# Seven block products for the long set's outputs, with their weights split ahead into DRAM, in an encoder layer on one Trainium2 core

## The chip, the core and the metric

The kernel runs on one core of a Trainium2 chip. A core has five engines with a queue of instructions each, which run beside one another and wait for each other through semaphores: TensorE (PE in the profile) does matrix products, VectorE (DVE) and ScalarE (ACT) do element-wise work on up to 128 rows at once, GpSimd (POOL) does element-wise work too, and SyncE (SP) only starts transfers. Any of SP, ACT and POOL can start a transfer (DMA). An instruction that waits holds up all that stand behind it in its engine's queue. The metric is the device time of one execution in microseconds (us); the kernel before takes 2188.45 us, the median of three runs.

## The reference

One encoder layer in fp32 is applied to a long set of 1024 rows (`x_prompt`, called A in the code) and a short set of 512 rows (`x_sample`, called B), each of 1024 columns. Per set:

```
h      = rms_norm(x) * pre_w                       # row by row
cols   = h @ w_in                                  # 1024 -> 12304 columns
y_m    = mlstm(q, k, v, gates) * sigmoid(o) * silu(z)       # 1024 wide
y_a    = dilated_attention(3 groups of q, k, v) * silu(z_a) #  512 wide
merged = sig(g_A) * (y_m @ w_proj_m) + sig(g_B) * (y_a @ w_proj_a)
out    = merged @ w_out
x      = x + rms_norm(out) * post_w
```

Everything after the two mixers, so `y_m @ w_proj_m`, `y_a @ w_proj_a`, the gates, `merged @ w_out`, the norm and the sum with x, is called the outputs here. It is these of the long set that the change rewrites.

## The kernel before

Every fp32 operand of a product is **split** into a high part (a copy rounded to the type that TensorE takes at full rate) and a low part (operand less high part), and each product is three matmuls: high by high, high by low, low by high (`mm3`, L230). ScalarE makes high parts by a copy, VectorE low parts by a subtraction. A matmul is 128x128 by 128x512. A step of the output work is one `mm3`.

The program has stages, and TensorE's order in the later ones is written by the program itself.

1. The value columns of the long set come first.
2. **The pairs**: the other columns of the long set, two units of 128 columns at a time, as seven block products in place of eight (`unit_pair`, L788, in the order m1 m6 m2 m7 m5 m4 m3 on TensorE; a product is 12 matmuls, a pair 84). There are 38 pairs: 12 `att`, then four times conv, conv, gate, then 8 `zo`, 2 `az`, and 4 gate pairs at the end. The weights of a pair go into buffers `pw_raw` (a ring of 4) through SP, and are split into `phla` (a ring of 2: the operands of m1, m2, m6, m5) and `phlb` (a ring of 2: one buffer for m7 and m4, one for m3). The names `c`, `pu2` and `pu3` are the pair's sums, made by VectorE from the PSUM tiles `d` (L808 takes m2 and L809 m6, L819 takes m3, the last product). The order of ScalarE, VectorE, POOL and SP in this stage is set by a scheduler, from priorities and its own cost table.
3. **The short set's inputs**: its rows are transposed on TensorE (L348), split into `H0` to `H3` (L354 on ScalarE, L355 on VectorE), and multiplied by `w_in` unit by unit (`dense` tiles). Their weights arrive in `wraw0` and `wraw1`, and are split into three pairs of places `wh`, `wl` (L285, L296, L302). The low parts of the first three units are made by POOL. SP's order is the program's own.
4. **Mixers with fill**: mLSTM and attention of A and B run one after another, each laid out in rounds, and between the rounds the class `Fill` puts steps of the dense work: the short set's inputs, then the outputs of A and of B. `STEPS` says how many steps go into which mixer. The steps of A's outputs are 128 for `w_proj_m`, 64 for `w_proj_a` and 128 for `w_out`, in two halves of rows (`branches` and `final`). Beside them the split of the next half's rows of y_m and y_a is made by `along`, which advances a generator once in so many steps. From L2540 on weights are issued by POOL's queue.
5. The mixed attention of B (`combine`), B's own projection and its `w_out` close the program. The residual `x` is loaded (`xo`), VectorE multiplies and adds to it (L2271), and SP stores it.

## Time and profile before

| what | value |
|---|---|
| median of three runs | 2188.45 us (2188.39 to 2188.65) |
| span of the profiled execution, first to last instruction | 2185.1 us |
| what lies around that span, against the median run | 3.4 us |
| TensorE busy | 2173.5 us, 99% |
| VectorE, ScalarE, POOL busy | 1460.8, 1085.1, 704.2 us |
| moved by DMA | 395.62 MB, mean 181 GB/s |
| granted TensorE clock | 0.999 |

The span is the only time that the profiled execution has of its own, so the 3.4 us are the difference from the runs' median. In the tables of windows below, a row gives the busy time of each engine in a stretch of 50 us, and how many instructions it ran. In a timeline a row gives start, length, engine, line and names; what stands in brackets at its end is the idle time before the instruction and what ended it. A matmul's own length in the profile overlaps with the next one's, so what a matmul costs is read from the distance between starts, or from their number in a stretch. Line numbers are those of the kernel before; in the kernel after, the same statement stands some lines further down (L764 becomes L766, L296 becomes L298, L285 becomes L287, L354 becomes L356, L808 becomes L858, L2145 becomes L2202).

### The profile page before, as it was taken

To read this page: it belongs to the slowest core of one execution; us is meant where nothing else is said; L and a number is where in the kernel's file an instruction comes from. 1 tells how busy PE (TensorE), PEld (TensorE's weight loads), DVE (VectorE), ACT (ScalarE), POOL (GpSimd) and SP (SyncE) were. 2 spreads that over 40 slices of the span, in tenths; PEclk is the share of its full clock that TensorE was granted. 3 is DMA by queue.
4 is the path that set the end of the run, shared out by engine and by line. 5 is a ranking of instruction groups with operands and counts; after the bars stand their busy time and mean duration, and the time that the engine had idled before them with its cause. 6 is when DMAs were issued, how large, how long until landed. Compare 5 with 4: busy or idle time off the path is not lost.

```text
span 2185.1 us, 33611 instructions
## 1 busy us (share of the span) xinstructions
PE 2173.5 (99%) x11626; PEld 1857.3 (85%) x11626; DVE 1460.8 (67%) x2927; ACT 1085.1 (50%) x2228; POOL 704.2 (32%) x989
## 2 busy tenths in 40 slices
...
GB/s 139 193 139 73 146 162 144 227 110 116 107 115 114 75 82 97 135 216 261 202 164 225 175 167 262 240 241 196 203 233 278 248 288 205 229 261 187 242 240 106
DMA packets 205748, 395.62 MB, mean 181 GB/s; under 512 B 36393, under 2 KB 117993, under 8 KB 205578
## 3 DMA queue, kind: packets, MB, share of 16 engines
...
## 4 chain that ended last, share of the span: by engine, by line
PE 97%; DVE 1%; ACT 1%; DMA 1%; issue 0%; POOL 0%; DVEq 0%; POOLq 0%; ACTq 0%
PE d L233 14%; PE d L235 14%; PE d L234 14%; PE dense L233 13%; PE dense L234 13%; PE dense L235 13%; PE lg L1801 2%; PE pt L1831 2%; PE o L1874 1%; PE num L233 1%; PE num L235 1%; PE num L234 1%; PE num L1494 1%; PE o L1853 1%; PE a L1201 1%; PE kv L233 1%
## 5 line engine op out<-in xcount | busy, mean ns | idle before, releaser
L233 PE MATMUL dense<-H,wh 128*128 128x512 f32 x664 | 269.3, 406 | 0.0
L234 PE MATMUL dense<-H,wh 128*128 128x512 f32 x664 | 260.3, 392 | 0.0
L235 PE MATMUL dense<-H,wl 128*128 128x512 f32 x664 | 260.2, 392 | 0.0
L233 PE MATMUL d<-Hh,phla 128*128 128x512 f32 x608 | 236.5, 389 | 0.0
L235 PE MATMUL d<-Hh,phla 128*128 128x512 f32 x608 | 236.5, 389 | 0.0
L234 PE MATMUL d<-Hl,phla 128*128 128x512 f32 x608 | 236.5, 389 | 0.0
L302 DVE TENSOR_TENSOR wl<-wraw,wh 128x1024 fp32r<-128x1024 f32 (+1 forms) x121 | 150.8, 1248 | 57.9 <-ACT wh L296 57.8
L235 PE MATMUL d<-Hh,phlb 128*128 128x512 f32 x456 | 177.4, 389 | 0.0
L233 PE MATMUL d<-Hh,phlb 128*128 128x512 f32 x456 | 177.4, 389 | 0.0
L234 PE MATMUL d<-Hl,phlb 128*128 128x512 f32 x456 | 177.4, 389 | 0.0
L296 ACT ACTIVATE wh<-wraw 128x1024 fp32r<-128x1024 f32 (+1 forms) x124 | 128.1, 1036 | 62.1 <-PE dense L234 24.3
L235 PEld LDWEIGHTS dense<-H,wl 128*128 128x128 f32 x664 | 124.7, 188 | 28.1
L782 POOL TENSOR_TENSOR psum_w<-pw_raw 128x512 f32<-128x512 f32 x38 | 56.7, 1492 | 271.1 <-DMA pw_raw<-w_in 259.9
L1820 DVE CUSTOM_DVE_ANT_0 ls<-lg,bias 128x256 f32<-128x256 f32 (+2 forms) x240 | 78.7, 350 | 90.3 <-PE lg L1801 61.7
L233 PEld LDWEIGHTS dense<-H,wh 128*128 128x128 f32 x664 | 125.0, 188 | 16.4 <-issue 1.2
L234 PEld LDWEIGHTS dense<-H,wh 128*128 128x128 f32 x664 | 125.2, 189 | 14.7
L235 PEld LDWEIGHTS d<-Hh,phla 128*128 128x128 f32 x608 | 114.1, 188 | 23.7
L234 PEld LDWEIGHTS d<-Hl,phla 128*128 128x128 f32 x608 | 114.1, 188 | 23.7
L233 PEld LDWEIGHTS d<-Hh,phla 128*128 128x128 f32 x608 | 114.1, 188 | 23.7
L800 POOL TENSOR_TENSOR psum_w<-pw_raw,psum_w 128x512 f32<-128x512 f32 x38 | 49.3, 1298 | 254.2 <-DVE phla L764 254.2
L1824 ACT ACTIVATE ls<-ls,nm 128x256 f32<-128x256 f32 (+1 forms) x192 | 87.3, 456 | 70.2 <-DVE nm L1822 47.0
L233 PE MATMUL d<-v,Hh 128*128 128x484 f32 (+1 forms) x336 | 121.3, 361 | 0.1
...
## 6 DMA issues: line engine op xcount, KB each, us to landing
pw_raw<-w_in SPq DMA_DIRECT2D x76, 512.0 KB, 3.9
wraw<-w_in SPq DMA_DIRECT2D x63, 512.0 KB, 4.4
aqk_a<-pwk SPq DMA_DIRECT2D x32, 512.0 KB, 6.7
wraw<-w_pm POOLq DMA_DIRECT2D x24, 512.0 KB, 5.9
wraw<-w_out POOLq DMA_DIRECT2D x24, 512.0 KB, 3.7
Q<-aqk_a SPq DMA_DIRECT2D x20, 512.0 KB, 6.3
...
aqk_b<-sw SPq DMA_DIRECT2D x36, 256.0 KB, 7.2
```

Of the source, the lines that this page charges most:

```text
L233: nc.tensor.matmul(out, lh, rh, start=start, stop=False, **kw)
L234: nc.tensor.matmul(out, lh, rl, start=False, stop=False, **kw)
L235: nc.tensor.matmul(out, ll, rh, start=False, stop=stop, **kw)
L296: high = nc.scalar.activation(hi[:, :n], raw[:, :n], AF.Copy)
L302: low = (self.lows or nc.vector).tensor_sub(lo[:, :n], raw[:, :n], hi[:, :n].bitcast(F32))
L782: self.nc.gpsimd.tensor_add(s[:, 0], ws[1][:, 0], ws[1][:, 1])
L800: nc.gpsimd.tensor_sub(s[:, 1], wa[:, 1], s[:, 1])
L1201: nc.tensor.matmul(p[:, c - c0], kT[:, ct, c * P:(c + 1) * P], qT[:, ct, c * P:(c + 1) * P], start=ct == 0, stop=ct == 1)
L1801: nc.tensor.matmul(lg[:, hh], q[hh][:, qs], z.rearrange("p (n j) -> p n j", j=P)[:, pair], start=z is k[hh], stop=z is not k[hh])
L1820: nc.vector.tensor_tensor_reduce(out=ls[rows, hh], in0=ts["lg"][hh][rows, of], in1=bt[rows, hh, by], scale=1.0, scalar=NEG, op0=OP.add, op ...
L1824: self.held = self.held[-3:] + [nc.scalar.activation(ls[:, hh], ls[:, hh], AF.Exp, bias=nm[:, hh:hh + 1], accum_out=ot[:, 128 + hh:129 + hh])]
L1831: nc.tensor.transpose(pp[:, hh * nk + x], ts["ls"][:, hh, x * P:(x + 1) * P], self.ident)
```

## The change

The outputs of the long set are computed as seven block products each for `w_proj_m` and `w_out`, 512 rows by 512 columns by 512 deep, so that each takes 112 steps in place of 128; `w_proj_a` keeps its 64. The weights that these need (five quadrants' combinations, each split) are prepared in the pairs stage: `pre_quads` loads quadrants of both weight matrices, makes the combinations on POOL, splits them into a `phlb` buffer and writes both parts to a DRAM tensor `pre`; `pre_plain` does the same for the unchanged weights (`w_proj_a`, and B's own). Sixteen calls of the first kind stand behind the 8 zo, the 4 gate and the 4 last pairs, twenty of the second behind the others. In the output stage a unit's weights are two transfers of 512 KB from `pre` straight into a split place. The combinations of the operands (sums of row blocks, the jobs of `combined` in the code), their splits and the sums of the products are done by VectorE and ScalarE between the steps (`outputs`). The residual is no longer loaded: eight transfers from DRAM to DRAM copy `x_prompt` into `y_prompt` during the conv pairs, and the finished rows are added there by accumulating transfers on POOL's queue. `STEPS` is redistributed, and the split of B's rows (`branches`, L2202) now runs in every second step of the last 28 of the long set's `w_out`.

```diff
             self.fetch(len(self.ready) + 1)
-            self.ready.append(self.net.split_w(*self.raws[len(self.ready)]))
+            raw = self.raws[len(self.ready)]
+            self.ready.append(self.net.split_w(*raw) if raw else self.net.load_pre(self.srcs[len(self.ready)][1]))
             self.fetch(len(self.ready) + self.net.deep)
 
     def fetch(self, n):
         while len(self.raws) < min(n, len(self.srcs)):
-            self.raws.append(self.net.load_w(*self.srcs[len(self.raws)]))
+            src = self.srcs[len(self.raws)]
+            self.raws.append(self.net.load_w(*src) if len(src) != 2 else None)
 
...
+    def pre_split(self, x, units, sb, to):
+        nc, n = self.nc, x.shape[1]
+        hl = sb.tile([P, 2, 2, BLK], F32R, name="phlb", bufs=2)
+        nc.scalar.activation(hl[:, 0, :n], x, AF.Copy)
+        nc.vector.tensor_sub(hl[:, 1, :n], x, hl[:, 0, :n].bitcast(F32))
+        for j, u in enumerate(units):
+            y = hl.rearrange("p z a c -> p z (a c)") if to is None else hl[:, :, j]
+            dst = self.pre[u] if to is None else self.pre[u, :, :, to]
+            nc.sync.dma_start(dst.rearrange("z p c -> p z c"), y.bitcast(F32))
+    def pre_plain(self, u, src, sb):
+        w = sb.tile([P, 2, BLK], F32, name="pw_raw", bufs=4)
+        self.nc.sync.dma_start(w, src.rearrange("p (a c) -> p a c", a=2))
+        self.pre_split(w, [u], sb, None)
+    def pre_quads(self, i, sb):
+        nc, q = self.nc, self.a["w_q"]
+        u, c = i // 4, slice(i // 2 % 2 * BLK, (i // 2 % 2 + 1) * BLK)
+        at = lambda *js: [4 * QUADS.index(j) + u for j in js]
+        ws = []
+        for b in range(2):
+            w = sb.tile([P, 2, BLK], F32, name="pw_raw", bufs=4)
+            nc.sync.dma_start(w, q[2 * b:2 * b + 2, u, :, c].rearrange("q p c -> p q c"))
+            ws.append(w)
+        wa, wb = ws
+        s = sb.tile([P, 2, BLK], F32, name="psum_w", bufs=2)
+        nc.gpsimd.tensor_add(s[:, 0], wb[:, 0], wb[:, 1])
+        nc.gpsimd.tensor_sub(s[:, 1], s[:, 0], wa[:, 0])
+        if i % 2 == 0:
+            self.pre_split(wa, at(0, 1), sb, c)
+            self.pre_split(s, at(4, 5), sb, c)
+        else:
+            nc.gpsimd.tensor_sub(wb[:, 0], wa[:, 0], wb[:, 0])
+            nc.gpsimd.tensor_sub(wa[:, 1], wa[:, 1], s[:, 1])
+            self.pre_split(wb, at(6, 3), sb, c)
+            self.pre_split(wa[:, 1:], at(7), sb, c)
+    def load_pre(self, u):
+        hi, lo = self.wsplit.pop(0)
+        self.wsplit.append((hi, lo))
+        for z, x in enumerate((hi, lo)):
+            self.loaded = self.side.dma_start(x[:, :1024].bitcast(F32), self.pre[u, z])
+        return hi[:, :1024], lo[:, :1024]
...
+    def outputs(self, T, before):
...
+        def divide(into, key, at, x):
+            hi, lo = at
+            nc.scalar.activation(hi, x, AF.Copy)
+            sub(lo, x, hi.bitcast(F32))
+            into[key] = at
+        def third(k):
+            sub(M["a1"][:, k], M["b1"][:, k], M["a1"][:, k])
+        def second(k):
+            add(M["a0"][:, k], M["a0"][:, k], M["a1"][:, k])
...
+        def proj_m(weights):
+            fill = weights.__self__
+            ring = [M["even"], slots("H0") + slots("H1")]
+            for n in range(2):
+                gate(n)
+            u, x = four("H3"), None
+            pm = M["pm"] = {(0, 0): four("H2"), (0, 1): u}
+            uses = [(i, k) for i in range(7) for _ in range(4) for k in range(4)]
+            jobs = combined("m", ring, uses)
...
+            for i in range(7):
+                for g in range(2):
+                    w = weights()
+                    if t == 0:
+                        self.more_places(fill, [[self.ring.tile([P, RING], F32R, name=f"wraw{z}") for z in range(2)]])
+                    for j in range(2):
+                        ps = self.dense()
+                        for k in range(4):
+                            give(jobs, t)
+                            give(late, t)
+                            c = slice(j * S + k * P, j * S + (k + 1) * P)
+                            self.mm3(ps, (w[0][:, c], w[1][:, c]), made["m", i, k], k == 0, k == 3)
+                            if k == 3:
+                                evict(i, 2 * g + j, ps)
+                            t += 1
+                            yield
+            assert not jobs
+            give(late, t, 99)
...
+            def close(b, t, ys):
+                s = ss[b][:, t]
+                nc.vector.scalar_tensor_tensor(s[:, 5:6], s[:, 0:1], 4 * EPS * D, s[:, 1:2], op0=OP.add, op1=OP.add)
+                nc.gpsimd.tensor_tensor(s[:, 6:7], s[:, 5:6], self.mhalf[:, :1], op=OP.pow)
+                r0 = b * S + t * P
+                for h, y in enumerate(ys):
+                    c = slice(h * S, (h + 1) * S)
+                    nc.vector.scalar_tensor_tensor(y, y, s[:, 6:7], pw[:, c], op0=OP.mult, op1=OP.mult)
+                    nc.gpsimd.dma_start(T.y[r0:r0 + P, c], y, accum_op=OP.add)
...
+        units = self.along(before, begin, 1)
+        units.append(Unit([("pre", 4 * i + g) for i in range(7) for g in range(2)], proj_m))
+        units.append(Unit([("pre", PRE_A + i) for i in range(KT // 2)], proj_a))
+        return units, Unit([("pre", 4 * i + 2 + k) for i in range(7) for k in range(2)], final)
...
-        return (self.along(before, lambda: self.split(T, b, 0, [(odd, 0, 1), (odd, 2, 1)], yb, 2 if len(before) > 1 else 3), 3)
-                + self.along([Unit([(a["w_pm"][ct],) for ct in range(KT)], proj_m)],
+        return (self.along(before, lambda: self.split(T, b, 0, [(odd, 0, 1), (odd, 2, 1)], yb, 3), 2, 86)
+                + self.along([Unit([("pre", PRE_M + ct) for ct in range(KT)], proj_m)],
                              lambda: self.split(T, b, 8, [(1 - odd, 1, 2)], ya, 3), 4)
-                + [Unit([(a["w_pa"][ct],) for ct in range(KT // 2)], proj_a)])
+                + [Unit([("pre", PRE_A + ct) for ct in range(KT // 2)], proj_a)])
 
...
-STEPS = (316, 260, 192, 290, 86)
+STEPS = (316, 260, 192, (6, 4.5), 22, 57)
+QUADS = (0, 1, 5, 6, 3, 4, 7)
+PRE_M, PRE_A, PRE_O, PRE = 28, 36, 40, 48
...
+                        if kind in ("zo", "gate"):
+                            N.pre_quads(i if kind == "zo" else 8 + i // 2, sb)
+                        elif plain:
+                            N.pre_plain(*plain.pop(0))
+                        if kind == "conv":
+                            with tc.issue_after(N.split_end.ins):
+                                t = rows.pop(0)
+                                nc.sync.dma_start(A.y[P * t:P * (t + 1)], A.x[P * t:P * (t + 1)])
...
                     c = N.unit_pair(N.pair_weights(u, u + 1, sb)[0], H, sb, cp, ps)
+                    N.pre_quads(12 + j, sb)
...
-            finals = [N.final(*x) for x in ((A, 0), (A, 1), (B, 0))]
-            units = short[:-4] + N.branches(A, 0, 0, short[-4:])
-            units += N.branches(A, 1, 1, finals[:1]) + N.branches(B, 0, 0, finals[1:2]) + finals[2:]
+            last = N.final(B, 0)
+            first, final = N.outputs(A, short[-4:])
+            units = short[:-4] + first + N.branches(B, 0, 0, [final]) + [last]
...
-                fill.stage(STEPS[4], 3 * B.n + 6)
+                fill.stage(STEPS[4], 4)
                 fill(2)
                 next(mixed)
                 fill(2)
+                fill.stage(STEPS[5], 3 * B.n + 2)
```

Three places show how instructions move. Names with a number are one buffer each.

**SP's queue at the end of the pairs stage.** Before, the last loads of pair weights, then those of the short set's inputs (`wraw`):

```order
L777 DMA pw_raw_7019<-w_in 128x1024 [waits DMAHW3_49,Pool_49]
L777 DMA pw_raw_7021<-w_in 128x1024 [waits DVE_49]
L1039 DMA gb512_7161<-gb4 128x1 [waits DMAHW3_49,Pool_49]
L285 DMA wraw0_7146<-w_in 128x1024 [waits DMAHW4_49,PE_49]
L285 DMA wraw1_7147<-w_in 128x1024 [waits DMAHW5_49]
L285 DMA wraw0_7146<-w_in 128x1024 [waits DMAHW6_49,DMAHW4_49,Pool_49]
L285 DMA wraw1_7147<-w_in 128x1024 [waits DMAHW7_49,DMAHW5_49,Pool_49]
```

After, the splits of the last two calls of `pre_quads` are written out first (`phlb_7539`, `phlb_7544`):

```order
L799 DMA pre_82<-phlb_7397 128x2x512 [waits DMAHW6_49,DVE_49]
L799 DMA pre_82<-phlb_7397 128x2x512 [waits DMAHW7_49]
L799 DMA pre_82<-phlb_7539 128x2x512 [waits DMAHW0_49,DVE_49]
L799 DMA pre_82<-phlb_7539 128x2x512 [waits DMAHW1_49]
L799 DMA pre_82<-phlb_7544 128x2x512 [waits DMAHW2_49,DVE_49]
L1089 DMA gb512_7570<-gb4 128x1 [waits DMAHW4_49,DMAHW3_49,Pool_49]
L287 DMA wraw0_7555<-w_in 128x1024 [waits PE_49]
L287 DMA wraw1_7556<-w_in 128x1024 [waits DMAHW5_49]
L287 DMA wraw0_7555<-w_in 128x1024 [waits DMAHW6_49,DMAHW4_49,Pool_49]
```

The last `pre` write waits for VectorE's subtraction into `phlb_7544`, and the loads of `wraw` stand behind it.

**VectorE's queue around the split of m7's operand in a conv pair that follows a gate pair.** Before (`phlb_4172` is the operand, `d_4136` the last product of the pair ahead of it):

```order
L764 TENSOR_TENSOR phla_4179<-psum_w_4182,phla_4179 128x1024 [waits Activation_49]
L816 TENSOR_TENSOR c_4048<-pu3_4027,d_4120 128x512 [waits PE_49]
L764 TENSOR_TENSOR phlb_4172<-pw_raw_4176,phlb_4172 128x1024 [waits DMAHW4_49,Activation_49]
L819 TENSOR_TENSOR c_4047<-pu2_4026,d_4136 128x512 [waits DVE_49,PE_49]
L764 TENSOR_TENSOR phlb_4173<-psum_w_4182,phlb_4173 128x512 [waits Activation_49]
L832 SCALAR_TENSOR_TENSOR pwk_4152<-c_4047,cws_686,pwk_4152 128x1024 [waits DMAHW1_49,Activation_49]
```

After (`phlb_4132` is the operand; `d_4095` is the last product of the pair ahead, `d_4180` and `d_4167` are m2 and m6 of the operand's own pair; `phlb_4121` is the second split of the `pre_quads` call between the two):

```order
L869 TENSOR_TENSOR c_4006<-pu2_3985,d_4095 128x512 [waits DVE_49,PE_49]
L795 TENSOR_TENSOR phlb_4121<-psum_w_4113,phlb_4121 128x1024 [waits Activation_49]
L858 TENSOR_TENSOR c_4151<-pu2_4130,d_4180 128x512 [waits PE_49,Activation_49]
L859 TENSOR_TENSOR pu2_4130<-pu2_4130,d_4167 128x512 [waits DVE_49]
L766 TENSOR_TENSOR phlb_4132<-pw_raw_4136,phlb_4132 128x1024 [waits DMAHW7_49,DMAHW0_49,Activation_49]
L766 TENSOR_TENSOR phla_4289<-pw_raw_4285,phla_4289 128x1024 [waits DMAHW4_49,Activation_49]
```

The subtraction into the operand has moved from a place ahead of its pair's sums to one behind the sums with m2 and m6. The same order stands in four pairs, the three that follow the first three gate pairs and the one behind the first of the last four; in two of the four another `phla` subtraction is between.

**VectorE's queue behind the long set's last step.** Before, the split of B's rows (L2145) stands among the last steps of the projection ahead of `w_out`, here with other work of that stage:

```order
L302 TENSOR_TENSOR wl2_7153<-wraw0_7146,wh2_7152 128x1024 [waits DMASW3_49,Activation_49]
L2145 TENSOR_TENSOR V1b_19925<-sraw_7268,V0b_19924 128x512 [waits DMASW7_49,Activation_49]
L2145 TENSOR_TENSOR V1b_19925<-ymr0_17490,V0b_19924 128x512 [waits DMASW0_49,Activation_49]
L2220 TENSOR_TENSOR H3_18683<-mg_19911,H2_18682 128x512 [waits Activation_49]
L2145 TENSOR_TENSOR V1b_19925<-ymr1_17491,V0b_19924 128x512 [waits DMASW1_49,Activation_49]
L1725 COPY pts_19966<-pt_19965 128x256 [waits PE_49]
L2263 TENSOR_TENSOR sw0_7264<-dense_19920,postw_18670 128x512 [waits Activation_49]
```

After, its first three parts (`K1` from `X0`) stand just behind the sum with the last product of the long set (`dense_20687`), and after them come 23 rows: eight multiplications of finished rows by the norm's weight (L2450), and the weights and sums of B's mixed attention. Then:

```order
L2103 TENSOR_TENSOR X1_20414<-V0a_20412,cw8_20747 128x512 x2
L2202 TENSOR_TENSOR K1_20517<-ymr1_17898,X0_20516 128x512 [waits DMASW0_49,Activation_49]
L2202 TENSOR_TENSOR H1_20519<-sraw_7674,H2_20518 128x512 [waits DMASW4_49,DMASW3_49,DMASW6_49,DMASW1_49,Activation_49]
L2109 TENSOR_TENSOR X1_20414<-X1_20414 128x512 [waits DVE_49]
L2202 TENSOR_TENSOR H1_20519<-ymr0_17897,H2_20518 128x512 [waits DMASW2_49,Activation_49]
L2109 TENSOR_TENSOR X1_20414<-X1_20414 128x512 [waits DVE_49]
L2202 TENSOR_TENSOR H1_20519<-ymr1_17898,H2_20518 128x512 [waits DMASW5_49,Activation_49]
L2202 TENSOR_TENSOR H1_20519<-sraw_7674,H2_20518 128x512 [waits DMASW6_49,Activation_49]
```

The five other parts (`ymr1`, `sraw`, `ymr0`, `ymr1`, `sraw`) have moved behind those rows. The two last of them take rows whose loads stand on POOL's queue behind the eight accumulating transfers of `y_prompt`.

252 lines of the change are left out of this document (236 added, 16 removed).

## The prediction

> **What bounds the kernel now.** I read the page's first and fourth part, the waits of TensorE, and the windows of 50 us.
>
> ```profile
> span 2185.1 us, 33611 instructions
> PE 2173.5 (99%) x11626; PEld 1857.3 (85%) x11626; DVE 1460.8 (67%) x2927; ACT 1085.1 (50%) x2228; POOL 704.2 (32%) x989
> PE 97%; DVE 1%; ACT 1%; DMA 1%; issue 0%; POOL 0%; DVEq 0%; POOLq 0%; ACTq 0%
> ```
>
> ```profile
> PE d L2370 <- DMA Hh<-prew: 2.3, 1, 2.3
> PE d L476 <- ACT Hh L470: 0.5, 1, 0.5
> PE d L420 <- DVE u2b L417: 0.5, 1, 0.5
> PE d L235 <- DVE Hl L472: 0.4, 1, 0.4
> ```
>
> ```profile
> 650.00:700.00 50.00, 50.00 (x222) 41.42 (x221) 40.47 (x40) 22.22 (x23) 18.40 (x13) 1.00 0.35 124
> 750.00:800.00 50.00, 50.00 (x222) 41.42 (x221) 28.59 (x34) 18.42 (x20) 14.40 (x12) 1.00 0.21 74
> 950.00:1000.00 50.00, 50.00 (x286) 43.33 (x285) 26.90 (x52) 29.23 (x60) 15.84 (x33) 1.00 0.90 306
> 2050.00:2100.00 50.00, 49.79 (x227) 40.72 (x226) 41.45 (x86) 13.31 (x23) 22.24 (x39) 1.00 0.84 281
> ```
>
> TensorE is the bound. It waited 3.7 us in four places of the values stage, and after that no stretch shows a gap. In the rows of windows the columns are TensorE, weight loads, VectorE, ScalarE and POOL, each with its count, then clock, share of the DMA engines and GB/s. Two things follow. A matmul taken away is worth 50.00/222 = 0.225 us (0.227 between starts in the next part), not the 389 ns that groups list. And since nothing is idle, whatever makes TensorE wait is paid in full: there is no later wait that could shrink. VectorE has 9 to 21 us of 50 free in the stages that the change loads, so its sum of work will not bind. The question is order: who stands behind what.
>
> **The removal.** Each of the long set's two large products goes from 128 steps to 112, a step being three matmuls: 32 x 3 = 96 fewer.
>
> ```profile
> 953.93 0.39 PE L233 MATMUL d<-Hh,phlb 128*128 128x512 f32 x1
> ...
> 954.39 0.39 PE L235 MATMUL d<-Hh,phlb 128*128 128x512 f32 x1
> ```
>
> Two starts apart is 0.46, so with the window's 0.225 I take 0.226: 96 x 0.226 = **-21.7 us**. Splits of output weights that fall away on ScalarE and VectorE free engines that TensorE never waited for: 0.
>
> **Place 1, from the pairs to the short set.** The rows of before:
>
> ```profile
> 938.49 10.95 SPq L285 DMA_DIRECT2D wraw<-w_in  x4
> 943.20 1.06 ACT L296 ACTIVATE wh<-wraw 128x1024 fp32r<-128x1024 f32 x1 [4.10 <-DMA wraw<-w_in]
> 944.34 4.75 POOL L302 TENSOR_TENSOR wl<-wraw,wh 128x1024 fp32r<-128x1024 f32 x2 [10.13 <-ACT wh L296]
> 949.97 1.06 ACT L296 ACTIVATE wh<-wraw 128x1024 fp32r<-128x1024 f32 x1 [4.47 <-DMA wraw<-w_in]
> 954.82 0.69 DVE L819 TENSOR_TENSOR c<-pu,d 128x512 f32<-128x512 f32 x1 [2.03 <-PE d L235]
> 955.25 4.73 ACT L354 ACTIVATE H<-d,prew 128x512 fp32r<-128x512 f32 x8 [4.22 <-PE d L348]
> 958.03 0.48 PE L233 MATMUL dense<-H,wh 128*128 128x512 f32 x1
> ```
>
> The last pair ends at E = 954.78. The first weights were issued 16.3 us ahead of that, so all three high parts were made by 951.03, and the eight `H` copies (L354) ran at once: first dense matmul at E+3.25. After the change, `phlb_7544` takes the buffer that m3 of the last pair reads, so its ScalarE copy starts at E, its VectorE subtraction stands behind the sum with m3 (two times 0.69), and SP can write it at about E+1.4. Behind that write stand the gate bias and `wraw`: first load issued about E+2.1. From issue to the first copy took 943.20-938.49 = 4.7: E+6.8. The first low part on POOL (4.75/2 = 2.4, from 1.1 behind the copy's start) ends at E+10.3. The third load reuses the first buffer, so it waits for that, and 944.34+2.4 to 949.97 is 3.2: third copy at E+13.5, done at E+14.6. On ScalarE the eight `H` copies stand behind that third copy, and dense starts 958.03-955.25 = 2.8 after the first of them: E+17.4 in place of E+3.25, **+14.2 us**. From below: were the `H` copies early and only the first weights late, dense would start at about E+10.4, +7; from above, the 512 KB writes in flight could delay each load by half its 4.4 us (the group below), +18. I take the chain as it stands. The mLSTM loads behind (Q, K) are late by as much, and so is their user.
>
> **Place 2, pairs behind a gate pair.** TensorE's m7 needs its low part in its third matmul, 8.16 + 0.45 = 8.6 us after the pair's start S (three products of 2.72, 36 x 0.2267).
>
> ```profile
> 935.58 0.39 PE L233 MATMUL d<-Hh,phla 128*128 128x512 f32 x1
> ...
> 943.99 0.69 DVE L808 TENSOR_TENSOR c<-pu,d 128x512 f32<-128x512 f32 x1 [6.80 <-PE d L235]
> 944.72 0.69 DVE L809 TENSOR_TENSOR pu<-pu,d 128x512 f32<-128x512 f32 x1
> ```
>
> ```profile
> L764 DVE TENSOR_TENSOR phlb<-pw_raw,phlb 128x1024 fp32r<-128x1024 f32 x38 | 52.3, 1375 | 12.7 <-ACT phlb L763 12.7
> L764 DVE TENSOR_TENSOR phla<-psum_w,phla 128x1024 fp32r<-128x1024 f32 x38 | 46.3, 1218 | 2.3 <-ACT phla L763 2.3
> L800 POOL TENSOR_TENSOR psum_w<-pw_raw,psum_w 128x512 f32<-128x512 f32 x38 | 49.3, 1298 | 254.2 <-DVE phla L764 254.2
> ```
>
> VectorE starts the sum with m2 at S+8.4 and waits 6.8 us for it, so it arrives early and the wait is for the product. With that sum and the one with m6 now ahead of the operand's subtraction, this starts at about S+9.8 and ends at S+11.1 (1.22 to 1.38): m7 is late by 2.5 us. In two of the four pairs another 128x1024 subtraction (1.22) stands ahead, so 3.7. Sum 2 x 2.5 + 2 x 3.7 = **+12.4 us**; from below 0, should m7 ask for the low part later than I read, from above 4 x 5 = 20 with POOL beside.
>
> [...]
>
> The other pairs: for a zo pair the `pre` write frees the operand's buffer. m4 ends at S-2.72, copy and subtraction (1.06, 1.38) to about S+0.7, two writes; then copy and subtraction again by S+8.6 leaves 8.6-0.7-2.4 = 5.5 us for the writes, which took 2.6 (below): hidden. If their landing were 6.7, as the slowest 512 KB write there, seven pairs lose 1.2 each.
>
> **Place 3, behind the long set's last step F.** VectorE's rows:
>
> ```profile
> 2053.51 1.89 DVE L2050 TENSOR_TENSOR X<-V0a,cw 128x512 f32<-128x512 f32 x3
> 2055.32 1.41 DVE L2056 TENSOR_TENSOR X<-X 128x512 f32<-128x512 f32 x2
> 2065.85 0.75 DVE L2271 SCALAR_TENSOR_TENSOR xo<-sw,ss,xo 128x512 f32<-128x512 f32 x1
> 2066.51 0.75 DVE L2271 SCALAR_TENSOR_TENSOR xo<-mg,ss,xo 128x512 f32<-128x512 f32 x1
> ```
>
> ```profile
> wraw<-w_in SPq DMA_DIRECT2D x63, 512.0 KB, 4.4
> qk_a<-pwk SPq DMA_DIRECT2D x16, 512.0 KB, 2.6
> aqk_a<-pwk SPq DMA_DIRECT2D x32, 512.0 KB, 6.7
> ymr<-ym_b POOLq DMA_DIRECT2D x5, 256.0 KB, 5.1
> y_prompt<-xo SPq DMA_DIRECT2D x12, 256.0 KB, 5.1
> ```
>
> B's first unit needs eight low parts, each for 3 x 0.226 = 0.68 us of TensorE: unhindered it would end 6 us after F. On VectorE three of them come at once (to F+3.5), then eight multiplications of finished rows at 0.66 apart (5.3), six mixing products at 0.60 to 0.63 (3.7), two sums (1.2), a dozen small ones (2): the fourth part ends at F+16.3, the sixth at F+18. The seventh and eighth also wait for rows whose buffers the fourth and fifth free, and whose loads stand behind the eight accumulating transfers (all released by F+13): 16.3 + 0.5 + 3 to 5.1, copy and subtraction 1.2, so F+21 to F+23 and then 0.7: TensorE is done at about F+23 in place of F+6, **+17 us**. From below 10, if the mixing products run before the last products come; from above 20. In before these parts were made beside the projection ahead, and the eight multiplications beside B's projection.
>
> **The rest.** More transfers: 26 MB of loads, 48 MB of `pre` writes and 8 MB of copies over the pairs' 740 us are about 110 GB/s beside rows of 74 to 211, under the 306 that the core moved at 950: 0 (up to 12 by the zo case and late rows). An accumulating transfer isn't in the trace; by the plain store's 5.1 us and twice that it is off TensorE's path but at place 3. `pre` loads are two issues for one on POOL's queue, which loses its sums: 0. Sums on VectorE in the products of the projection and at `w_out`'s start: about 3 tiles whose eviction queues behind operand jobs, 1 us each, **+3** (0 to 6).
>
> **Sum.** 2185.1 - 21.7 + 14.2 + 12.4 + 17 + 3 = 2210.0, and with the 3.4 us around the span **2213.4 us**.
>
> **Rivals.** (a) VectorE isn't late: its rows at places 2 and 3 are reached before TensorE asks, because the sums and multiplications ahead of them find their inputs ready. It decides once VectorE's block behind F is under 5 us and m7's part is done by S+8.6. Then 2188.5 - 21.7 + 14.2 = 2181, faster. For it: the free 9 to 21 us of 50. Against it: VectorE's 6.8 us of idle ahead of m2's sum, so it waits for the product, not the reverse. (b) Place 3 alone is hidden, the others stand: 2196. For it: the rows' squares and norms come on other engines and may be early; against it the hand sum of VectorE's rows. (c) Transfers turn into a bound: `pre` writes land late in seven zo pairs (8 us at 6.7) and POOL's queue brings weights late in the output stage, where the DMA share was already 0.84: 2213 + 12 = 2226. Against it: 281 GB/s was moved there with no wait of TensorE. (d) The stalls come at about half, and 2188 to 2192 is left.
>
> **How the numbers follow.** Forecast 0.55, (a) 0.18, (b) 0.10, (c) 0.12, (d) 0.05. Four fifths of (d) and nothing else is within 0.2% (4.4 us, about what a measurement of this kernel can tell from no change): same 0.04, faster 0.19, slower 0.77. The forecast's own range is 2202 to 2222; the range for 8 in 10 goes down to (a) and up to (c): 2181 to 2228.
>
> **What would show it.** Right: waits of TensorE in the profile after, one of 14 us ahead of the first dense tile with ScalarE's `H` named, four of 2 to 4 us on `phlb` from VectorE, and one or more on B's split rows. Their sum is what the matmuls' 21.7 is to be held against. Wrong: no wait at the dense tile (SP's order doesn't bind there), or TensorE's waits naming weights (`wh`, `sw`) from transfers, which is (c).

## The result, and the profile after

| | before | after |
|---|---|---|
| time, median | 2188.42 us | 2301.46 us (2296.72 to 2304.98) |
| ratio | | 1.0519, 95% interval 1.0504 to 1.0534 |
| span of the profiled execution | 2185.1 us | 2303.0 us |
| TensorE's waits, sum of all rows | 3.7 us | 100.4 us |
| granted clock, mean of the span | 0.999 | 0.975 |
| first pair matmul to first transposes (38 pairs) | 723.6 us | 801.3 us |
| from there to the first dense matmul | 3.4 us | 18.4 us |
| first `lg` matmul to the end | 883.0 us | 904.6 us |

The change is slower by 113 us, where the forecast said 25. From the first `lg` (products of the attention) to the end lie all of the 96 matmuls that fell away, so it should have become 21.7 us shorter; it became 21.6 longer. The page of the kernel after (busy times, and the chain that ended last):

```profile
span 2303.0 us, 33946 instructions
...
PE 2194.3 (95%) x11530; PEld 1858.2 (81%) x11530; DVE 1527.5 (66%) x3015; ACT 1087.9 (47%) x2252; POOL 798.0 (35%) x1081
...
PE 75%; DMA 8%; DVE 7%; issue 4%; ACT 3%; POOL 1%; SPq 0%; DVEq 0%; POOLq 0%; ACTq 0%
```

The 96 matmuls are gone (11626 to 11530), and yet TensorE is busy for 21 us more: the same instructions ran slower. The chain, of which TensorE had 97%, now leads through transfers and VectorE. TensorE's waits (total, times, longest):

```profile
PE d L235 <- ACT phlb L765: 48.7, 10, 10.1
PE d L350 <- DVE H L357: 14.0, 1, 14.0
PE dense L236 <- DVE K L2202: 7.2, 2, 3.9
PE dense L235 <- ACT X L2201: 5.6, 1, 5.6
PE dense L235 <- ACT H L2201: 5.0, 1, 5.0
PE dense L235 <- DMA wh<-pre: 3.4, 2, 2.8
PE lg L1851 <- DVE ot L1870: 3.3, 1, 3.3
PE d L237 <- DVE phlb L766: 2.7, 5, 0.8
```

Half of it is one row that I had not forecast: ScalarE's copy into `phlb`, the operand of a pair, ten times. And waits are not all. Windows around one of them (behind the window stand its length and TensorE's busy time; third from the end is the granted clock, then DMA share and GB/s):

```profile
528.00:530.00 2.00, 0.00 (x0) 0.00 (x0) 0.00 (x0) 0.00 (x0) 1.92 (x3) 1.00 1.05 420
530.00:531.00 1.00, 0.00 (x0) 0.00 (x0) 0.00 (x0) 0.00 (x0) 1.00 (x1) 0.64 1.03 404
...
534.00:536.00 2.00, 2.00 (x6) 1.53 (x5) 1.17 (x2) 0.34 (x1) 0.00 (x0) 0.50 0.76 252
...
538.00:540.00 2.00, 2.00 (x10) 1.68 (x9) 0.44 (x1) 0.00 (x0) 0.00 (x0) 1.00 0.00 0
```

TensorE's last matmul ahead of the wait ends at 526.05. From 530.3 the clock is at half, and it stays so for 5 us after TensorE has resumed at 532.23. The trace holds 14 such stretches (one more at the very end, as before), 112.6 us together, and TensorE was busy in them for 68.0. So the balance of the two spans is 2185.1 - 21.7 + 96.7 (waits) + X = 2303.0, with X = 43 us for what a wait costs beside its length: a remainder, which the run with timed waits takes apart below.

**Place 1**, the rows of the step from the pairs to the short set, in the timeline of the kernel after:

```profile
1033.27 2.12 SPq L799 DMA_DIRECT2D pre<-phlb  x3
...
1036.20 11.07 SPq L287 DMA_DIRECT2D wraw<-w_in  x4
...
1041.13 1.06 ACT L298 ACTIVATE wh<-wraw 128x1024 fp32r<-128x1024 f32 x1 [6.86 <-DMA wraw<-w_in]
...
1047.70 1.06 ACT L298 ACTIVATE wh<-wraw 128x1024 fp32r<-128x1024 f32 x1 [4.28 <-DMA wraw<-w_in]
1048.66 4.72 ACT L356 ACTIVATE H<-d,prew 128x512 fp32r<-128x512 f32 x8
...
1051.79 0.78 PE L235 MATMUL dense<-H,wh 128*128 128x512 f32 x1
```

The last pair ends at E = 1033.6. Behind it TensorE begins the transposes (`d`, L350) and stands 14.0 us in them, until VectorE has split `H` (L357). First copy at E+7.5 (forecast 6.8), third at E+14.1 (13.5), `H` copies behind it at E+15.1 (14.6), dense at E+18.2 (17.4).

**Place 2**, the pair behind the first gate pair:

```profile
521.03 1.06 ACT L2770 ACTIVATE c<-c 128x1024 f32<-128x1024 f32 x1 [4.71 <-DVE c L866]
522.00 1.04 ACT L794 ACTIVATE phlb<-psum_w 128x1024 fp32r<-128x1024 f32 x1
...
531.12 1.06 ACT L765 ACTIVATE phlb<-pw_raw 128x1024 fp32r<-128x1024 f32 x1 [6.12 <-DMA pre<-phlb]
...
522.48 4.06 SPq L799 DMA_DIRECT2D pre<-phlb  x4
...
532.23 0.80 PE L235 MATMUL d<-Hh,phlb 128*128 128x512 f32 x1 [6.18 <-ACT phlb L765]
```

ScalarE makes the second operand for `pre` at 522.0 (the gate's tanh, L2770, stands ahead and waited for the pair's last sums). Its write is issued until 526.5, and the buffer is the one that the next pair's operand gets. ScalarE stands 6.1 us for the landing, and so does TensorE. The four pairs of the forecast took 8.9, 14.6, 8.5 and 9.4 us more than before, 41.4 together; other pairs, from the first zo pair on, lost the 36 that are left.

**Place 3**, behind the long set's last step (F = 2151):

```profile
2157.16 0.69 DVE L2202 TENSOR_TENSOR K<-ymr,X 128x512 fp32r<-128x512 f32 x1 [1.79 <-DMA V0a<-og_b]
...
2168.81 1.90 DVE L2103 TENSOR_TENSOR X<-V0a,cw 128x512 f32<-128x512 f32 x3
2170.62 0.68 DVE L2202 TENSOR_TENSOR K<-ymr,X 128x512 fp32r<-128x512 f32 x1
...
2166.54 0.22 ACT L2089 ACTIVATE cw<-cw 128x24 f32<-128x24 f32 x1 [11.36 <-DVE cw L2088]
2166.66 0.61 ACT L2201 ACTIVATE X<-ymr 128x512 fp32r<-128x512 f32 x1
...
2179.45 0.63 ACT L2201 ACTIVATE H<-ymr 128x512 fp32r<-128x512 f32 x1 [11.13 <-DMA ymr<-ym_b]
...
2157.57 0.54 POOL L835 DMA_DIRECT2D wh<-pre  x1 [0.73 <-DMA y_prompt<-K]
...
2158.84 0.59 POOL L276 DMA_DIRECT2D ymr<-ym_b  x1
...
2171.61 0.57 POOL L276 DMA_DIRECT2D ymr<-ym_b  x1 [0.49 <-DVE K L2202]
```

B's first unit is done at about F+32 where I had F+23: four waits on its parts (17.8 us by the list above) and clock. Each wait has its own end. The first, 3.9 us, ends when the accumulating transfer out of `K` has landed (`y_prompt<-K`, at 2157.0; VectorE's row puts it down to another transfer, POOL's names it). The second, 5.6, ends with VectorE's row L2088: behind it stand ScalarE's small copy L2089 and then the copy of B's rows, whose loads had landed half a us before. The third, 3.2, is VectorE's subtraction at 2170.62, behind eight multiplications and the mixing. The fourth, 5.0, is the last rows: asked for at 2171.61, when that subtraction had freed their buffer, and landed 7.8 us later.

### The profile page after: what moved, and what is told of

Its sections match the earlier page's. It is cut to its first block, busy times and chain, and to the rows that moved or that the text cites. A ratio compares the mean times of both kernels' runs of the same rounds, so it can differ in the third digit from the quotient of the medians.

```text
span 2303.0 us, 33946 instructions
## 1 busy us (share of the span) xinstructions
PE 2194.3 (95%) x11530; PEld 1858.2 (81%) x11530; DVE 1527.5 (66%) x3015; ACT 1087.9 (47%) x2252; POOL 798.0 (35%) x1081
## 4 chain that ended last, share of the span: by engine, by line
PE 75%; DMA 8%; DVE 7%; issue 4%; ACT 3%; POOL 1%; SPq 0%; DVEq 0%; POOLq 0%; ACTq 0%
PE dense L235 11%; PE dense L236 11%; PE dense L237 11%; PE d L237 9%; PE d L235 9%; PE d L236 9%; DMA pre<-phlb 4%; PE lg L1851 2%; DVE pwk L882 2%; PE pt L1881 1%; DMA pw_raw<-w_in 1%; DVE phlb L795 1%; PE o L1924 1%; PE num L235 1%; PE num L237 1%
## 5 line engine op out<-in xcount | busy, mean ns | idle before, releaser
L235 PE MATMUL d<-Hh,phlb 128*128 128x512 f32 x456 | 185.7, 407 | 48.7 <-ACT phlb L765 48.7
L237 PE MATMUL d<-Hh,phlb 128*128 128x512 f32 x456 | 185.2, 406 | 2.9 <-DVE phlb L766 2.7
L236 PE MATMUL d<-Hl,phlb 128*128 128x512 f32 x456 | 183.8, 403 | 0.0
L235 PEld LDWEIGHTS d<-Hh,phlb 128*128 128x128 f32 x456 | 89.4, 196 | 70.7 <-ACT phlb L765 52.9
L236 PEld LDWEIGHTS dense<-H,wh 128*128 128x128 f32 x656 | 124.7, 190 | 14.6
L304 DVE TENSOR_TENSOR wl<-wraw,wh 128x1024 fp32r<-128x1024 f32 (+1 forms) x86 | 108.0, 1257 | 30.2 <-ACT wh L298 30.2
L237 PE MATMUL d<-v,Hl 128*128 128x484 f32 (+1 forms) x336 | 120.6, 359 | 0.4 <-DVE Hl L474 0.4
```

Source lines behind the costliest of these rows:

```text
L235: nc.tensor.matmul(out, lh, rh, start=start, stop=False, **kw)
L236: nc.tensor.matmul(out, lh, rl, start=False, stop=False, **kw)
L237: nc.tensor.matmul(out, ll, rh, start=False, stop=stop, **kw)
L304: low = (self.lows or nc.vector).tensor_sub(lo[:, :n], raw[:, :n], hi[:, :n].bitcast(F32))
```

## The experiments

Each run is compared with the kernel before on the same chip. "Pairs" is the time from the first pair matmul to the first transposes: 723.6 us before, 801.3 after.

**A third buffer in the ring**, paid for with one buffer of sums, one work tile and a narrower scratch tile:

```diff
-        bs = [sb.tile([P, 2, 2, BLK], F32R, name="phlb", bufs=2) for _ in range(2)]
+        bs = [sb.tile([P, 2, 2, BLK], F32R, name="phlb", bufs=3) for _ in range(2)]
...
-        hl = sb.tile([P, 2, 2, BLK], F32R, name="phlb", bufs=2)
+        hl = sb.tile([P, 2, 2, BLK], F32R, name="phlb", bufs=3)
```

> One edit with its make-room: the ring phlb gets three buffers in place of two, so that the first operand of a pair no longer takes a buffer whose pre write has yet to land. Room comes from psum_w (one buffer for two), the work tiles (three for four) and a two-byte scratch tile for the short set's norm. All transfers stay. Theory (a buffer of the shared ring is free only when its pre write has landed, 7 us from issue): the ten waits for ScalarE's phlb (48.7 us) and the half clock behind seven of them go, a pair takes 19.04 us again, the run falls by about 75 to about 2226 (2218 to 2240). Rival 1 (the core's transfers as such are the limit, about 400 GB/s in those stretches): the waits turn to pair weights and the run stays above 2275. Rival 2 (place 2 of the prediction: VectorE's order alone): only four pairs gain, 12 to 25 us, 2277 to 2290.

2271.09 us, ratio 1.0384 (1.036 to 1.0408); pairs 780.5. TensorE's rows on `phlb` are gone, and 36 us of waits on `phla`, the pair's other operand, stand in their place. ScalarE still stood 163 us of the stage ahead of copies into `phlb`, for writes to land. So more depth moved the wait; it did not take it away, and the forecast of 2226 was 45 us off. It is not depth alone, since the room came from other rings: ScalarE also stood 74 us ahead of copies into `phlb` for sums on POOL, whose tile had lost a buffer.

**Only the higher halves written**, and loaded twice:

```diff
-            dst = self.pre[u] if to is None else self.pre[u, :, :, to]
-            nc.sync.dma_start(dst.rearrange("z p c -> p z c"), y.bitcast(F32))
+            dst = self.pre[u, 0] if to is None else self.pre[u, 0, :, to]
+            nc.sync.dma_start(dst, y.bitcast(F32))
```

> Only the high part of each prepared weight is written to DRAM, and the output stage loads the high part twice, so the low parts of the output weights are left out of the computation: half the bytes of pre writes, ring and order of the after kernel as they are. Theory (landing of the writes sets the end of the wait): writes land in 4 to 5 us in place of 7, each wait at the pairs shrinks by about 3, so 48.7 us become 15 to 25 and most of the half clock goes: 2301 - 40 = about 2260 (2245 to 2275). Rival 1 (transfers as such): the same direction, told apart by third_buffer. Rival 2 (VectorE's order): no change, 2295 to 2305.

2248.99 us, 1.0281 (1.0266 to 1.0296), pairs 746.0: the forecast was 11 us off. The run leaves out the lower parts of the output weights. It can't tell a buffer that is held for less time from fewer bytes in flight.

**The last four quadrant jobs two pairs earlier** (two az pairs and the first two GB pairs in place of the four GB pairs):

```diff
+                        elif kind == "az":
+                            N.pre_quads(12 + i // 2, sb)
...
-                    N.pre_quads(12 + j, sb)
+                    if j < 2:
+                        N.pre_quads(14 + j, sb)
```

> The last four calls of pre_quads move up: two stand behind the az pairs, which had none, and two behind the first two of the last four pairs, so that nothing of pre stands ahead of the short set's weights on SP's queue. Theory (place 1: SP's order): the 14.0 us wait ahead of the first dense tile and the half clock behind it go, about 17 us: 2284 (2278 to 2292), with the pairs' waits moved but not fewer. Rival (ScalarE's order, H copies behind the third weight copy, or the loads' landing): dense still starts 8 us or more behind the last pair, and the gain is under 8.

2283.38 us, 1.0439 (1.0422 to 1.0457). From the transposes to dense it is 3.4 us again, as before the change, and TensorE's wait of 14.0 us is gone. Place 1 is this chain.

**Row buffers and places at the end**: five more buffers for rows, and the places of B's lower halves exchanged for ones that the accumulating transfers don't hold.

```diff
-        return self.four((("X0", "K1", "H2", "H1"), ("V0b", "K0", "V1b", "Q1"))[which][i], dt)
+        return self.four((("X0", "K0", "H2", "Q1"), ("V0b", "K1", "V1b", "H1"))[which][i], dt)
...
+            N.rows_in += [end.tile([P, BLK], F32, name=f"ymx{i}") for i in range(5)]
```

> B's row parts at the end of the long set: five more row buffers (so that all eight rows are loaded without waiting for an earlier part), and their low parts go where the odd operands of w_out stood (K0, Q1) and no longer where its first finished rows stand (K1, H1), whose accumulating transfers have to land first. Theory (place 3 is a chain of row loads and landings, three buffers at a time, 8 us a turn): five waits of 19.6 us between 2153 and 2180 and the half clock among them shrink to about 5: 2301 - 20 = about 2281 (2274 to 2288). Rival (VectorE's 20 us of work, as predicted): parts still wait their turn behind the multiplications and mixing sums, gain under 8: above 2293.

2285.89 us, 1.0447 (1.0431 to 1.0463). The four waits of place 3 are gone. But VectorE's order changed with them: B's last part now stands ahead of the eight multiplications, which stood ahead of five parts before.

```profile
2153.86 0.68 DVE L2202 TENSOR_TENSOR Q<-ymx,H 128x512 fp32r<-128x512 f32 x1
...
2156.86 2.73 DVE L2450 SCALAR_TENSOR_TENSOR H<-H,ss,postw 128x512 f32<-128x512 f32 x4
```

So the run doesn't part the landings from VectorE's rows. Other waits appear, the first of them on the mixing of the short set (total, times, longest):

```profile
PE tp L2114 <- DVE ss L2445: 6.4, 1, 6.4
PE dense L235 <- DMA wh<-pre: 4.1, 2, 3.9
```

**A buffer of its own for the small operand** (the one for the product m3; 4 KB a partition, half of it paid with the second buffer of the tile `pu2`):

```diff
-        bs = [sb.tile([P, 2, 2, BLK], F32R, name="phlb", bufs=2) for _ in range(2)]
+        bs = [sb.tile([P, 2, 2, BLK], F32R, name="phlb", bufs=2), sb.tile([P, 2, 1, BLK], F32R, name="phls", bufs=1)]
```

> The operand of m3, which fills half of a phlb buffer, gets a buffer of 4 KB of its own (phls), so that the two phlb buffers alternate between a pair's first operand and the prepared splits; room comes from one pu2 tile for two, and the rings of pair weights, work tiles and psum_w stay as they are in the kernel after. All transfers stay. Theory (a buffer is free only when its pre write has landed; what third_buffer still lost came from the work tiles it gave up): pairs take 19.04 us, no wait on phlb, phla or c above 1 us, the stage falls from 801 to about 725 us, the run by 70 to 78 to 2223 to 2232. Rival (the transfers as such): waits of 20 us and more stay in the pairs, on phla or on pair weights, and the run is above 2245.

2277.27 us, 1.0406 (1.039 to 1.0421), pairs 785.4: far off. TensorE's waits moved to `phla` (34.9 us). ScalarE's copies into `phlb` still stand for writes (behind the bar: idle time ahead, and what ended it):

```profile
L794 ACT ACTIVATE phlb<-pw_raw 128x1024 fp32r<-128x1024 f32 (+1 forms) x44 | 42.8, 972 | 28.9 <-DMA pre<-phlb 16.4 <-PE d L237 12.4
L765 ACT ACTIVATE phlb<-pw_raw 128x1024 fp32r<-128x1024 f32 x38 | 40.3, 1060 | 144.9 <-DMA pre<-phlb 105.9 <-issue 9.6 <-PE d L237 7.6
```

**These three together** (small operand, quadrant jobs, rows):

> own_small, quads_early and rows_ahead together: all that the change does, with the three kinds of waits taken away. Theory (the three places and the half clock behind their waits are all that eats the gain of 21.7 us): 2301 - 76 - 18 - 16 = about 2191 (2180 to 2200), with the rest in the waits left by rows_ahead (6 to 9 us), one of 3.3 at B's attention and 3.4 on weights at the end. Rival (transfers of the output stage or the sums on VectorE cost TensorE elsewhere): above 2205.

2253.27 us, 1.0296 (1.0281 to 1.0312), pairs 785.5. The gains one by one (24.2, 18.1 and 15.6 us) would make it 2243.6. The pair stage keeps a loss of 62 us: a buffer for the small operand alone does not take it away.

**Made waits in the kernel before**, by holding back the second weight load of five pairs:

```diff
-            with self.tc.high_priority():
+            with self.tc.high_priority(), ExitStack() as st:
+                if after is not None and u == ub:
+                    st.enter_context(self.tc.issue_after(after.ins))
```

> The kernel before, with five waits made: in five att pairs the second load of weights is issued only behind the sum with m5, m4 or m3 of the pair ahead (m5, m4, m3, m4, m3 in turn), so that TensorE waits at m6 for about 2, 4, 7, 4, 7 us. Nothing else differs. Theory (a wait of about 3 us or more is followed by about 5 us at half clock, which costs 2.5 to 3 beside the wait): pairs with the longer waits take their wait and 2.5 to 3 more, the shorter only its wait; 24 + 4 x 2.7 = about 35, so 2223. Rival (a wait costs itself alone): 2188 + 24 = 2212, and the pair's length less 19.04 is the wait.

2188.27 us, 1.0002 (0.9992 to 1.0011): no wait arose, each pair took 19.04 us. The two loads of a pair were still issued together, 1.5 us later than before, and were needed most of a pair later. It tells nothing of a wait's price.

**Timed waits in the kernel before**, by work on VectorE instead:

```diff
+        for _ in range(slow):
+            nc.vector.scalar_tensor_tensor(a22[1], m5.rearrange("p (k c) -> p k c", k=4), 0.0, a22[1].bitcast(F32),
+                                           op0=OP.mult, op1=OP.add)
         m4 = product(T4, a22)
```

> The kernel before with five made waits of TensorE: in every second attention pair from the third on, 1, 2, 3, 5 and 8 additional VectorE instructions (0.69 us each: lo = 0 x product + lo) stand between the product with T1 and the lower half that the next product needs. By VectorE's two sums ahead of them TensorE should wait 1.8, 2.5, 3.2, 4.5 and 6.6 us, 18.6 us in all. Granted clock (a wait of some 3 us is followed by some 7 us at half clock, which costs 2.5 to 3 us more): the pairs with 1 and 2 additional ones are longer by their wait alone, those with 3, 5 and 8 by 2.5 to 3 us more: 2188.4 + 18.6 + 8.2 = 2215 us. No price of its own: every pair is longer by its wait, 2207 us, and the granted clock stays 1.0.

2218.77 us, 1.0143 (1.0127 to 1.0158). The rows of the five waits in TensorE's timeline:

```profile
285.05 0.50 PE L235 MATMUL d<-Hh,phlb 128*128 128x512 f32 x1 [1.53 <-DVE phlb L816]
...
326.68 0.50 PE L235 MATMUL d<-Hh,phlb 128*128 128x512 f32 x1 [3.26 <-DVE phlb L816]
...
370.66 0.80 PE L235 MATMUL d<-Hh,phlb 128*128 128x512 f32 x1 [3.99 <-DVE phlb L816]
...
416.90 0.80 PE L235 MATMUL d<-Hh,phlb 128*128 128x512 f32 x1 [5.43 <-DVE phlb L816]
...
464.46 0.79 PE L235 MATMUL d<-Hh,phlb 128*128 128x512 f32 x1 [7.61 <-DVE phlb L816]
```

| wait | the pair is longer by | above the wait | half clock left behind the resume |
|---|---|---|---|
| 1.53 | 1.82 | 0.3 | 0 |
| 3.26 | 5.17 | 1.9 | 3.41 |
| 3.99 | 6.71 | 2.7 | 5.23 |
| 5.43 | 7.31 | 1.9 | 3.36 |
| 7.61 | 9.58 | 2.0 | 3.59 |

The kernel has nothing else changed, so the third column is what a wait costs beside its length. It has two parts. The wait of 1.53 us left the clock at 1.00 and still cost 0.3, which I take for the restart. Behind the four others the clock was at half for some us more, and matmuls stood 0.43 us apart there in place of 0.227:

```profile
328.66 0.63 PE L233 MATMUL d<-Hh,phlb 128*128 128x512 f32 x1
329.09 0.63 PE L234 MATMUL d<-Hl,phlb 128*128 128x512 f32 x1
```

So a us at half clock loses 0.47 us of work. By 0.3 and 0.47 times the last column the four would cost 1.9, 2.8, 1.9 and 2.0 (estimates), against 1.9, 2.7, 1.9 and 2.0 measured: the price hardly grows with the wait, it goes by what is left of the half clock when TensorE resumes. The same two parts for the changed kernel are 0.47 x 68.0 = 32 us for its 14 stretches and 0.3 x 30 = 9 for the 30 waits that it has more than the kernel before: 41 us by estimate, and its remainder was 43.

**Tiny writes**, 8 partitions of 128, so a sixteenth of the bytes (the halves are loaded from those eight rows):

```diff
-            y = hl.rearrange("p z a c -> p z (a c)") if to is None else hl[:, :, j]
+            y = hl[:8].rearrange("p z a c -> p z (a c)") if to is None else hl[:8, :, j]
```

> The changed kernel with each `pre` write cut to 8 of its 128 partitions (a sixteenth of the bytes); the loads of halves read those eight rows sixteen times, so they move the bytes that they moved (the result is then not the reference's). ScalarE's copies, VectorE's subtractions, GpSimd's sums, the buffers and the orders stay. Held buffers (a buffer of the ring `phlb` is not free before its write has landed, 7.1 us in the median, and ScalarE's queue stands behind the copy that wants it): the writes now land in about 2 us, the rows 'ACT phlb' and 'DVE phlb' of TensorE's waits go, the 38 pairs take 19.04 us but for a few, and the time falls by the 78 us that the pair stage lost: 2224 us (2215 to 2240). Bytes in flight (the writes make the loads of the next weights late): the same. Engines (VectorE is 17.4 to 17.7 us busy of a pair's 19.0 in the conv and gate pairs and cannot take the splits): the pair stage stays long, 2280 or more.

2310.75 us, 1.056 (1.0539 to 1.058). As a whole the run says little, since loads that read the same eight rows land late at the end (9.1 and 10.4 us for `wh` and `wl`, where the changed kernel's took 5.6 and 5.9). The pair stage is what it was made for: 768.3 us, and the first three pairs behind gate pairs lose 8.6, 8.9 and 7.9 us (8.9, 14.6 and 8.5 with full writes). ScalarE's groups there:

```profile
L765 ACT ACTIVATE phlb<-pw_raw 128x1024 fp32r<-128x1024 f32 x38 | 40.3, 1061 | 75.8 <-PE d L237 43.7 <-DMA pre<-phlb 29.2 <-POOL psum_w L819 2.4
...
L765 ACT ACTIVATE phlb<-psum_w 128x512 fp32r<-128x512 f32 x38 | 23.9, 630 | 37.6 <-DMA pre<-phlb 31.3 <-POOL psum_w L850 2.6 <-POOL psum_w L819 2.0
```

A write of 32 KB still holds its buffer for some us: at 523.75 to 526.5 it was issued behind two loads of 512 KB in the same queue, and ScalarE got the buffer at 529.4, 2.9 us after the issue (4.6 with full writes). What the landing of so small a write is made of stays open.

**Free writes**: full bytes, taken from a tile that never changes, so that no write holds the ring.

```diff
-            y = hl.rearrange("p z a c -> p z (a c)") if to is None else hl[:, :, j]
+            y = self.fixed.rearrange("p (z a) c -> p z (a c)", z=2) if to is None else self.fixed[:, :2]
```

> The changed kernel with every `pre` write at its place, of its size and behind nothing, but its bytes taken from one operand tile of the pairs that stays in place for the whole stage (the result is then not the reference's). The split still runs into the ring, and no write holds the ring. It tells the two apart that the run with tiny writes cannot. Held buffers: the pair stage is free of loss as there, 2224 us (2215 to 2240). Bytes in flight: the loads of pair weights and of the quadrants still land late behind 48 MB of writes, and the stage keeps most of its loss: 2270 to 2300.

2319.71 us, 1.0607 (1.0592 to 1.0623), and a run that went elsewhere than meant: with nothing to wait for, the writes were issued among those of the values, before the pairs, and TensorE waited 79.6 us there. The pairs behind it, with all splits on ScalarE and VectorE in place, took 726.2 us: nothing held, no bytes of `pre` in the stage, hardly any loss. That ends the theory that the engines' work is too much.

**Free writes in place**: the bytes now come from the pair's own output, which exists only when the pair is done. The edit also moves the `pre` work behind the pair's own use of that output (not shown).

```diff
-            y = hl.rearrange("p z a c -> p z (a c)") if to is None else hl[:, :, j]
+            y = self.fixed.unsqueeze(1).to_broadcast([P, 2, 2 * BLK]) if to is None else self.fixed.rearrange("p (z c) -> p z c", z=2)
```

> The run with writes that hold nothing, mended: there the writes, with nothing to wait for, were sent in the stage of the values, 80 us ahead of the pairs. Now each `pre` write takes its bytes from the pair's own output tile `c` (three buffers, two used a pair), so that it can't be sent before the pair is done, and the pre work stands behind the pair's use of it; the splits still run into the ring, and no write holds the ring (the result is then not the reference's). Bytes and transfers of the stage are those of the changed kernel. With the run with tiny writes (hold without bytes: the pair stage took 768.3 us), the changed kernel (both: 801.3) and the run with writes ahead (neither: 726.2) it makes the fourth corner. Bytes cost only by way of the hold: 732 us (726 to 740), and 2301 - 69 = 2232 us in all. Bytes cost by themselves, as much as between the changed kernel and tiny writes: 726 + 33 = 759 us, 2259 in all. Bytes are the whole: 790 or more.

2242.97 us, 1.025 (1.0233 to 1.0267), pairs 737.2. Its writes landed after 8.1 and 6.9 us, as slowly as the changed kernel's 7.2 and 7.6, and 222 GB/s were moved in the stage (204 in the changed kernel). ScalarE's copies no longer wait for any of them:

```profile
L765 ACT ACTIVATE phlb<-pw_raw 128x1024 fp32r<-128x1024 f32 x38 | 40.2, 1057 | 41.4 <-DVE phlb L795 22.3 <-PE d L237 12.8 <-issue 6.3
...
L765 ACT ACTIVATE phlb<-psum_w 128x512 fp32r<-128x512 f32 x38 | 23.5, 618 | 15.4 <-POOL psum_w L850 7.5 <-DVE phlb L795 6.2 <-PE d L237 1.7
```

Where the changed kernel has, in the same groups:

```profile
L765 ACT ACTIVATE phlb<-pw_raw 128x1024 fp32r<-128x1024 f32 x38 | 40.3, 1060 | 90.7 <-DMA pre<-phlb 44.3 <-PE d L237 40.3 <-DMA pw_raw<-w_pm 3.4
...
L765 ACT ACTIVATE phlb<-psum_w 128x512 fp32r<-128x512 f32 x38 | 24.0, 631 | 69.2 <-DMA pre<-phlb 64.3 <-PE d L237 3.3 <-POOL psum_w L785 1.6
```

With the ring and the splits the same (the place of the `pre` work too, but for the free writes in place), that makes a table of five kernels:

| | ScalarE stood for writes in `phlb` | pairs | lost against 723.6 |
|---|---|---|---|
| changed kernel | 108.6 us | 801.3 | 77.7 |
| tiny writes | 60.5 | 768.3 | 44.7 |
| higher halves alone | 46.8 | 746.0 | 22.4 |
| free writes in place | 0 | 737.2 | 13.6 |
| free writes (sent ahead) | 0 | 726.2 | 2.6 |

Full bytes with nothing held cost 11 us more than no bytes; held buffers cost 42 us with hardly any bytes, and 64 with all of them. The 42 come from two kernels that differ in the writes alone, so in this ring the hold is what costs; that bytes count mostly by making it longer rests on the run that also moved the `pre` work. ScalarE's standing is no price in itself: with three buffers and with a buffer for the small operand it stood longer (163 and 153 us), and the stage lost less than in the changed kernel (57 and 62).

**One operand a pair**, the three mends, with the plain units loaded raw again and the mixing spread over more steps:

```diff
-                        if kind in ("zo", "gate"):
-                            N.pre_quads(i if kind == "zo" else 8 + i // 2, sb)
...
+                        if kind != "gate":
+                            N.pre_half(halves.pop(0), sb)
```

> All three mends of the run before it (own small buffer for m3's operand, no pre work in the last two pairs, row buffers and places of the end), and the pre work thinned: one split operand a pair, in the attention, conv, zo and az pairs and the first two pairs behind, none in the four gate pairs (the sums of a quadrant pair are made from a second load of it); the 20 plain units are loaded raw again and split on ScalarE and GpSimd beside the later stages as the kernel before does it; the mixing of the short set at the end is spread over 80 steps of dense work instead of 57. With one pair operand and one pre operand a pair, two buffers alternate: a pair's operand never waits for a landing, and a pre operand waits for one that was issued 19 us before. Held buffers: 19.04 us a pair as in the twelve attention pairs of the changed kernel, which have just this load; 2188.4 - 21.7 + 1.0 + some 5 at the start of the dense work + some 8 at the end = 2181 us (2174 to 2192), the first kernel of these below the one before. Bytes or engines: the conv triples go on losing 7 us each, and the zo pairs two: 2215 to 2235.

2280.32 us, 1.0425 (1.0408 to 1.0443), pairs 787.3. I had taken two buffers and two users in turn for two separate buffers. The addresses of the tiles in the built program, in order of use, show that they aren't:

```
phlb_1946  137472  pair's operand
phlb_2089  145664  pre operand
phlb_2116  145664  pair's operand
phlb_2244  137472  pre operand
phlb_2271  137472  pair's operand
```

Each pair's operand takes the buffer of the `pre` operand ahead of it, whose write has just been issued. And with raw units the end, from the first `lg`, takes 21.8 us more than with the three mends; one wait there is of 4.1 us, for a lower half from POOL.

**Rings of their own** for the pair's operand and for the `pre` operand, else as the run before:

```diff
-        hl = sb.tile([P, 2, 2, BLK], F32R, name="phlb", bufs=2)
+        hl = sb.tile([P, 2, 2, BLK], F32R, name="phlp", bufs=1)
```

> The run with one operand a pair, and one edit: the pre operand has a ring of its own (one buffer, `phlp`), the pair's operand for the products with T3 and T4 another (one buffer, `phlb`), where both shared two buffers. The buffers' addresses show why one operand a pair did not help: the scheduler gives a pair's operand the buffer that was released last, which is that of the pre write just issued, so each pair's copy waited for the landing of the write ahead of it, and never took the other buffer. Bytes, engine work and memory stay. Held buffers: TensorE's waits for `phla` and `phlb` go (below 5 us in all), the pair stage takes 727 us (723 to 735) instead of 787, and the time falls by these 55 to 60 us, to 2222 us (2215 to 2232). Bytes or engines: the pair stage stays at 770 or more and the time above 2262.

2294.19 us, 1.0482 (1.0466 to 1.0498), pairs 799.4: wrong by its sign. No copy waits for a write any more. But the scheduler now sets the `pre` copies as early as their buffer allows, and ScalarE waits 103 us for their weights and sums. It stands still longer ahead of the pair's own small operand, for its sum on POOL:

```profile
L765 ACT ACTIVATE phls<-psum_w 128x512 fp32r<-128x512 f32 x38 | 24.0, 630 | 248.0 <-POOL psum_w L847 245.8 <-PE d L237 2.2
...
L794 ACT ACTIVATE phlp<-pw_raw 128x1024 fp32r<-128x1024 f32 (+1 forms) x32 | 30.5, 953 | 103.2 <-POOL pw_raw L824 37.3 <-POOL pw_raw L816 28.1 <-POOL pw_raw L819 24.2
```

**Held buffers kept apart**: whole quadrant jobs again, higher halves in a ring of 4 KB buffers, lower halves in place of the loaded weight, weights of `pre` in two buffers of their own; the pairs keep two buffers of weights in place of four, and one `phlb`.

```diff
+        hi, lo = sb.tile([P, 2, BLK], F32R, name="phi", bufs=2), x.bitcast(F32R)
...
-            w = sb.tile([P, 2, BLK], F32, name="pw_raw", bufs=4)
+            w = sb.tile([P, 2, BLK], F32, name="pq_raw", bufs=2)
```

> All three mends (the run of that name, whole quadrant pairs at their places, all 48 units split into DRAM), with what a landing holds kept apart from what the pairs use: the higher half of a pre operand goes into a ring of its own (two buffers of 4 KB), the lower half takes the place of the loaded weight, the loaded weights of the pre work have two buffers of their own and the pairs' weights two, and the pair's operands one buffer each; the mixing of the short set is spread over 80 steps of dense work, and the sums of the quadrants of y_m stand 8 steps later behind their loads. Bytes and VectorE's and ScalarE's work are those of the changed kernel. Held buffers: the pair stage takes 730 us (724 to 745; the scheduler now takes the pre work up to a pair earlier, two a pair beside the attention pairs, whose transfers had 0.72 of the DMA engines already) instead of 785, the waits of 6.9, 1.5 and 3.3 us at the end go with some 5 us of half clock, and the time is 2253 - 55 - 15 = 2183 us (2175 to 2200). Bytes or engines: the pair stage stays above 765 us, the time above 2225.

2245.99 us, 1.0258 (1.0241 to 1.0275), pairs 768.6: the best version that computes everything, and far from the 2183 expected. No copy waits for a write here either. TensorE waits for `phla` (24.3 us by VectorE's half, 5.6 by ScalarE's), and ScalarE's row has the same form as in the run before:

```profile
L794 ACT ACTIVATE phi<-pq_raw 128x1024 fp32r<-128x1024 f32 (+1 forms) x52 | 51.6, 992 | 148.4 <-POOL pq_raw L828 47.7 <-POOL pq_raw L821 36.2 <-DMA pq_raw<-w_pm 19.6
```

**Loads a pair ahead** of the copies that need them:

```diff
+                        if jobs and not last:
+                            next(jobs[0])
```

> The run with the held buffers kept apart, and one edit: the weights of a pre job are loaded a pair before they are split (the next job's loads stand behind the split of the job ahead), and its copies and subtractions stand behind the pair's own last split. In the run before, TensorE's waits for `phlb` were gone, but it still waited 24 us for VectorE's and 6 us for ScalarE's halves in `phla`; there ScalarE's queue stood for 2.3 and 4.7 us before copies of pre operands whose loads from w_q had been issued 7 to 9 us earlier and had just landed. Held queues (any instruction of the pre work that waits for a landing, a write's or a load's, holds the pair's own splits behind it in ScalarE's and VectorE's queues): with the loads 19 us ahead these waits go too, the pair stage takes 735 us (725 to 750) instead of 769, and the time is 2246 - 34 = 2212 us (2198 to 2228). Bytes in flight alone (48 MB more of writes make the pairs' own loads late, wherever the pre work stands): 765 us or more, and 2240 or above.

2258.2 us, 1.0316 (1.0298 to 1.0333), pairs 782.5. The edit did not do what it says: the loads stand behind writes that must land on SyncE's queue, so they were issued some 3 to 12 us, not 19, ahead of their use, and ScalarE stood longer than ever:

```profile
L795 ACT ACTIVATE phi<-pq_raw 128x1024 fp32r<-128x1024 f32 (+1 forms) x52 | 51.6, 993 | 199.0 <-DMA pq_raw<-w_pm 54.2 <-POOL pq_raw L831 43.8 <-DMA pq_raw<-w_q 38.0
```

It tells nothing against the theory and nothing for it beyond that row. So the last three runs took the held buffers away and did not get the time back. What they have in common is argued, not separated: an instruction of the `pre` work that waits, for a landing load or a sum on POOL, holds the pair's own splits behind it in ScalarE's queue. Fewer buffers for the pair's own operands and weights, which all three have, could do it too.

## Why the prediction was right or wrong

The sign was right (0.77 on slower), the time 88 us short and outside the range. By its terms:

- **96 matmuls, -21.7.** The count is as said. Its worth was not measured by itself; with it the balance above closes to within 2 us of the estimate of what waits cost.
- **Place 1, +14.2: right.** Measured 15.0 (18.4 against 3.4), each step within 0.8 us (the wait of 14.0 stands at a transpose and not at dense), and the run with earlier quadrant jobs takes it away.
- **Place 2, +12.4: failed.** The pair stage lost 77.7, of it 52.3 waits and the rest half clock and restarts; the four pairs of the forecast alone lost 41.4. Two steps failed. "With that sum and the one with m6 now ahead of the operand's subtraction" named VectorE's order; in the trace VectorE waits for ScalarE's copy, and that for a landing. And "5.5 us for the writes, which took 2.6 (below): hidden" took 2.6 us from one group of stores (`qk_a`) where 7.2 and 7.6 were to come; I had 6.7 in the row below it and used it for a rival alone, at 1.2 us a pair. Even that bound was too small, because the copy that waits is not the last thing lost: the pair's next splits stand behind it in the same queue (with three buffers TensorE's waits stood on `phla`, 36 us). The free writes in place show that the landing costs by way of the buffer: landings as slow, and 13.6 us lost in place of 77.7.
- **Place 3, +17: right in size for the waits (17.8), in its cause only in part.** I added up VectorE's rows, and the second and third wait (5.6 and 3.2 us) do end with them, though the loads had landed only half a us before the second ended. The two others end with landings: that of an accumulating transfer, which held a place, was not in the sum, and the late loads, which I had as a second condition at 3 to 5.1 us, took 7.8. No run parts the two causes. The half clock among the waits is on top: done at F+32, not F+23.
- **The rest, +3.** Waits on evictions came to 0.7 us. In its place stand 3.3 us at an `lg` of B's attention and 3.4 on weights, which I had at 0. In the run of the three mends VectorE stood 10.2 us shortly ahead of that `lg` for the loads of `y_m`'s quadrants; 8 steps more between the loads and the sums (in the run with buffers kept apart) left 9.6 there, and a wait of 4.3, so its cause is not settled.
- **A term that was missing: what a wait costs beside its length, 43 us.** "Whatever makes TensorE wait is paid in full" was too little: by the run with timed waits some 32 us of it are half clock and some 9 restarts (estimates above). The 14 stretches at half clock in the changed kernel's trace last 3.4, 6.8, 10.2, 13.7 or 17.1 us. What starts one is not settled: single waits of 3.26 us (timed waits) and 2.8 (changed kernel) were followed by one, and so were two of 1.45 and 0.53 that stood 0.7 us apart, at 1018.5; two of 1.51 and 0.53 as far apart, at 996.9, were not, nor was the single one of 1.53 in the timed waits. I had no such term, because the longest wait in the trace of before, 2.3 us, left the clock at 1.00.
- **The rivals.** (c) had the mechanism, `pre` writes that land late, at 12 us instead of some 78. It was held against it that 281 GB/s had been moved without a wait; but in the changed kernel's pairs, at a mean of 204 GB/s, `qk_a` landed in 2.6 us and `pre` in 7.2, so the rate did not tell the time of one transfer, nor who stood behind it. By the signs that I gave, "four of 2 to 4 us on `phlb` from VectorE" was wrong at first sight: ten of up to 10 us, from ScalarE.
- **VectorE beside POOL.** The 1.3 us a pair that "4 x 5 = 20 with POOL beside" allows for it were my estimate from the length of one of POOL's sums before (1298 ns); no run shows it for those four pairs. In the changed kernel a subtraction that met POOL's sum took 2.31 us in place of 1.22, the median; the sum beside it took 2.16, where the one ahead of that, which met no subtraction of a split, took 1.29:

```profile
510.56 1.29 POOL L784 TENSOR_TENSOR psum_w<-pw_raw 128x512 f32<-128x512 f32 x1 [3.07 <-DVE phlb L766]
511.93 2.16 POOL L785 TENSOR_TENSOR psum_w<-psum_w,pw_raw 128x512 f32<-128x512 f32 x1
...
512.86 2.31 DVE L766 TENSOR_TENSOR phla<-pw_raw,phla 128x1024 fp32r<-128x1024 f32 x1
```

That is 1.1 us lost by this one; the mean of its row, 1.4 us, hid it. TensorE's waits for VectorE's halves in the stage came to 3.6 us, so it was not what the stage lost.
